# Decoder trunk with a top-2-of-8 expert layer: five steps of the last expert move behind the branch, and a small overflow block goes from two array tiles to four

## The chip, the cores and the metric

The kernel runs on one core of one Trainium2 chip. The time is in device microseconds (us) of one execution of the program; of several runs the median is given. A profile of one execution says what each engine did and when: PE is TensorE's matmul, PEld its weight load, DVE VectorE, ACT ScalarE, POOL GpSimd, and SP issues the weight loads (DMA).

## The reference

Two decoder layers work on 256 tokens of width 1024, all in float32. Each layer mixes tokens (mLSTM beside a short gated convolution) and then channels: a dense SwiGLU in the first layer, eight experts in the second. The change touches only the experts:

```python
logits = (t @ w_router).astype(jnp.float32)
top_v, top_i = lax.top_k(logits, TOP_K)
probs = jax.nn.softmax(top_v, axis=-1)
gates = (jax.nn.one_hot(top_i, N_EXPERTS, dtype=jnp.float32) * probs[..., None]).sum(-2)
out = jnp.zeros_like(t)
for e in range(N_EXPERTS):
    out = out + gates[:, e, None].astype(t.dtype) * swiglu(t, w13[e], w2[e])
```

with `swiglu(h, w13, w2) = (silu(a) * b) @ w2`, where `a` and `b` are the halves of `h @ w13`. Every expert has 3584 hidden columns: 29 MB of `w13` and 15 MB of `w2`. So the layer reads 352 MB of weights, whatever the routing.

## The kernel before

**Units, steps, parts.** Weights come in units of 1 MB (128 x 2048 float32), each loaded by SP into one buffer of a ring of seven (`load`, L112). An expert is worked in seven steps of 512 hidden columns. A step has two up parts (a and b, two units each) and a down part (two units). In a light expert the two up parts are one ("up", four units).

**Two ways to multiply.** An expert with up to 128 tokens is *wide* ("split"): ACT rounds each half unit to float32r (`hi`, L119), DVE takes the remainder (`lo`, L121), and TensorE makes three passes of 512 columns (L472 to L474). A *light* expert with up to 64 tokens is "plain": its weights are used raw in float32, and `side_by_side` (L1068) puts two matmuls beside each other in the array, each with 64 tokens as rows of the result and one half of the columns. A float32 matmul shows as two instructions in the trace. The activations are turned by TensorE (L1103), and a finished expert is scaled and added to the sum (`combine`, L1139 to L1151).

**Which expert goes which way.** The last expert (here e7) does not wait for the ranking: it runs wide, all seven steps, ahead of a branch (L1385), while DVE ranks the other seven by load. The branch chooses one of six ways from these loads. The profiled program takes the first: e0, the most loaded, has more than 128 tokens, so 128 of them are a wide block and the rest, the *overflow*, a second block of 64 slots with two array tiles; e1 is wide; e2 to e6 are light. For each of e0's half units the wide passes and the overflow's matmuls follow each other, on the same weights.

**What sets the order.** `ranked` (L1307) writes one list of parts: light parts, with heavy ones (e0, then e1) put in after light down parts by a cost per part, 4 for e0's and 1 for e1's, spread to the end. This gives the order of loads, conversions (up to five half units ahead) and matmuls in the program; the compiler's scheduler still moves instructions of one engine against each other. The code after the branch exists once for every way.

Of the kernel before, what the change touches and what calls it, by code (L numbers as in the profile page):

```python
# [14 lines left out]
OP = mybir.AluOpType  # L15
# [18 lines left out]
AHEAD = 4  # L34
NR = NE - 1
# [9 lines left out]
def trunk(ctx: ExitStack, tc: tile.TileContext, x, c, w_ada, b_ada, w_in, w_gates, b_gates, conv_qk,  # L45
# [85 lines left out]
    using = [None]  # L131


    def fits():
        live = [x[2] for x in loaded] + [x[3] for x in made if x[3]] + [x for x in using if x]
        return bool(plan) and (not live or loads[0] + 1 - min(live) < len(turns["raw"][1]))
# [685 lines left out]
    def moe(ctx, norms, gb, Gc, Bc, l, g1):  # L822
# [30 lines left out]
        slots = [const.tile([128, 128], F32, name=f"slots{i}") for i in range(3)]  # L853
# [3 lines left out]
        G.iota(slots[2].rearrange("p (a b) -> p a b", a=2), pattern=[[0, 2], [1, 64]], base=-int(OFF),  # L857
               channel_multiplier=0, allow_small_or_imprecise_dtypes=True)
# [62 lines left out]
        def order():  # L921
# [38 lines left out]
            V.scalar_tensor_tensor(most, most, 5.0, few[:, 0:1], op0=OP.mult, op1=OP.add)  # L960
# [23 lines left out]
        class Block:  # L984
            def __init__(self, hi, lo, place, ready=None):
                self.hi, self.lo, self.place, self.side, self.ready = hi, lo, place, lo is None, ready
# [79 lines left out]
        def side_by_side(o, act, w, n, start, stop):  # L1066
            for c in range(2):
                T.matmul(o[c * 64:c * 64 + 64, 0:n], act, w[:, c * n:c * n + n], start=start, stop=stop)  # L1068

        def activations(b):  # L1070
            if b.side:
                return small.tile([128, 256], F32, tag="ss", bufs=4, name="ss")
            return small.tile([128, 512], F32, tag="ms", bufs=2, name="ms")


        def up(xs, s):
# [3 lines left out]
            for k2, (whi, wlo, raw) in enumerate(w for _ in range(2) for w in unit(3)):  # L1080
                for b, src in zip(xs, srcs):
                    for kk in range(2):
                        k = k2 * 2 + kk
                        if b.side:
                            side_by_side(src, b.hi[:, k], raw[:, kk], 256, k == 0, k == KC - 1)
                        else:
                            passes(src, b.hi[:, k], b.lo[:, k], whi[:, kk], wlo[:, kk], k == 0, k == KC - 1)
# [9 lines left out]
        def turned(xs, s):  # L1097
            out_ = []
            for b, s_ in zip(xs, s):
# [4 lines left out]
                if b.lo is None:  # L1104
                    ghi, glo = small.tile([128, n, 128], F32, tag="mg", bufs=3, name="mg"), None
# [8 lines left out]
        def ybanks(xs):  # L1114
            return [bank() if b.side else [bank(), bank()] for b in xs]

        def down(xs, j, ys, gs_):
            for u in range(2):
                for kk, (whi, wlo, raw) in enumerate(unit(3)):
                    cc, first, last_ = u * 2 + kk, j == 0 and u + kk == 0, j == STEPS - 1 and u + kk == 2  # L1120
                    for b, y, (ghi, glo) in zip(xs, ys, gs_):
                        if b.side:

                            side_by_side(y, ghi[:, kk, u * 64:u * 64 + 64], raw[:, 0], 512, first, last_)
                            continue
                        for hf_ in range(2):
                            hs = slice(hf_ * 512, hf_ * 512 + 512)
                            passes(y[hf_], ghi[:, cc], glo[:, cc], whi[:, 0, hs], wlo[:, 0, hs], first, last_)
                    if bits:
                        bits.popleft()()  # L1130
# [5 lines left out]
        def combine(b, y, gs, DT):  # L1136
            ys = next_ys()
            if b.side:
                V.scalar_tensor_tensor(ys[:, 0], y, gs, g1_halves, op0=OP.mult, op1=OP.mult)  # L1139
            for hf_ in range(0 if b.side else 2):  # L1140
                V.scalar_tensor_tensor(ys[:, hf_], y[hf_], gs, g1[:, hf_ * 512:hf_ * 512 + 512], op0=OP.mult,
                                       op1=OP.mult)

            def add(tb):
                pos_ = [bank() for _ in range(2)]
                for hf_, po in enumerate(pos_):
                    ps = slice(hf_ * 64, hf_ * 64 + 64) if b.side else slice(0, 128)
                    T.matmul(po, DT[ps, tb * 128:tb * 128 + 128], ys[ps, 0 if b.side else hf_], start=True, stop=True)
# [64 lines left out]
        def parts_of(*exs):  # L1213
            steps = [(ex, j) for ex in exs for j in range(STEPS)]
# [10 lines left out]
        def run(parts, at):  # L1225
# [7 lines left out]
            for ex, j, what in parts:  # L1233
# [5 lines left out]
                if what in ("up", "up b"):  # L1239
# [3 lines left out]
                    if (ex, j) in at:  # L1243
                        at[ex, j]()
            bits_left(0)
# [40 lines left out]
        g1_halves = h4("g1_halves", F32, (128, 512))  # L1286
# [3 lines left out]
        for c in range(2):  # L1290
            A.copy(g1_halves[c * 64:c * 64 + 64], g1[c * 64:c * 64 + 64, c * 512:c * 512 + 512])
# [13 lines left out]


        def ranked(x_0, x_6, narrow):  # L1307
            restore(early)
# [199 lines left out]
```

## Time and profile before

| what | value |
|---|---|
| median of 3 runs | 1810.29 us (1809.36 to 1810.42) |
| profiled execution | 1809.25 us, span of its instructions 1807.5 us |
| granted TensorE clock, mean | 0.987 |
| TensorE busy | 1714.5 us (95%) |
| DVE / ACT busy | 1046.7 / 727.4 us |
| read from memory | 538.20 MB, 298 GB/s over the span |
| expert weights | 336 loads of 1024 KB on SP's queue |

A row of a group reads: line, engine, operation, what is written from what, shapes, count, then busy time, mean of one in ns, and the idle time ahead of it with its cause. Matmuls are pipelined: a row's length is that of one instruction through the array, and the next one starts before it ends, so throughput is read from the distance between starts.

### The profile page before, as it was taken

The numbers are of one execution on the slowest core, as the hardware profiler recorded it, in microseconds if no ns is written. First come the engines' busy times: TensorE is split into PE (matmuls) and PEld (weight loads), VectorE is DVE, ScalarE is ACT, GpSimd is POOL, SyncE is SP. The second block draws the span as 40 slices with busy tenths as digits, with TensorE's granted clock in tenths as the row PEclk, the third lists the DMA queues.
The fourth block names the chain that finished last, engine by engine and source line by source line (L and its number), as shares of the span: only waits on it lengthen the run. The fifth ranks groups of instructions, "written<-read, shape, count | busy, mean of one in ns | idle before, by whom it ended". The sixth has DMA issues, their size and how long they took to land. (4 is left out here: it accounts for less than half of the span.)

```text
span 1807.5 us, 27089 instructions
## 1 busy us (share of the span) xinstructions
PE 1714.5 (95%) x10848; PEld 1285.7 (71%) x10848; DVE 1046.7 (58%) x1524; ACT 727.4 (40%) x971; POOL 69.8 (4%) x80
## 2 busy tenths in 40 slices
PE   5999998999998999997999999999999999999996
PEld 4899996999996999995776555454554455566763
DVE  7699857866659999669887112222222222364645
ACT  2764544444434855446765112122121211244541
POOL 0002002000003001002000000000000000000000
PEclk8999999999999999998999999999999999999998
DMA  8666753866664677654886999999998999999993
GB/s 347 214 255 243 270 184 115 307 252 231 232 234 176 235 277 282 231 187 152 338 292 234 367 411 369 386 352 400 364 398 318 394 366 381 404 372 415 421 421 149
DMA packets 78126, 541.10 MB, mean 299 GB/s; under 512 B 10056, under 2 KB 10408, under 8 KB 13224
## 3 DMA queue, kind: packets, MB, share of 16 engines
q1 hardware_dynamic: 74880, 534.81, 76.3%
q10 hardware_dynamic: 3112, 4.48, 0.7%
q8 instruction: 87, 1.43, 0.3%
q14 instruction: 47, 0.39, 0.1%
HBM read 538.20 MB, written 1.05 MB: 298 GB/s over the span
## 5 line engine op out<-in xcount | busy, mean ns | idle before, releaser
L121 DVE TENSOR_TENSOR lo<-raw,hi 128x1024 fp32r<-128x1024 f32 x382 | 457.9, 1220 | 177.6 <-ACT hi L119 176.1
L119 ACT CAST hi<-raw 128x1024 fp32r<-128x1024 f32 x388 | 399.3, 1049 | 304.0 <-PE grp L461 184.2
L460 PE MATMUL grp<-h_hi,hi 128*128 128x256 f32 x1408 | 401.8, 286 | 0.5 <-ACT hi L119 0.5
L462 PE MATMUL grp<-h_hi,lo 128*128 128x256 f32 x1408 | 397.7, 283 | 0.0
L461 PE MATMUL grp<-h_lo,hi 128*128 128x256 f32 x1408 | 397.5, 282 | 0.0
L460 PEld LDWEIGHTS grp<-h_hi,hi 128*128 128x128 f32 x1408 | 268.6, 191 | 2.9 <-issue 1.4
L461 PEld LDWEIGHTS grp<-h_lo,hi 128*128 128x128 f32 x1408 | 268.6, 191 | 2.0 <-issue 1.7
L462 PEld LDWEIGHTS grp<-h_hi,lo 128*128 128x128 f32 x1408 | 268.4, 191 | 0.0
L1093 DVE TENSOR_TENSOR ss<-bank,ss 128x256 f32<-128x256 f32 x42 | 17.8, 425 | 308.8 <-PE bank L1068 301.4
L472 PE MATMUL bank<-hi,x_parts 128*128 128x512 f32 x336 | 138.9, 413 | 2.8 <-ACT hi L119 2.8
L474 PE MATMUL bank<-lo,x_parts 128*128 128x512 f32 x336 | 133.9, 399 | 1.8 <-DVE lo L121 1.8
L473 PE MATMUL bank<-hi,x_parts 128*128 128x512 f32 x336 | 132.2, 393 | 0.0
L1091 ACT ACTIVATE ss<-bank 128x256 f32<-128x256 f32 x42 | 16.1, 384 | 277.1 <-PE bank L1068 277.1
L1068 PE MATMUL bank<-raw,x_pairs 128*64 128x256 f32 x1024 | 117.1, 380 | 0.0
L1068 PE MATMUL bank<-raw,mg 128*64 128x512 f32 x432 | 115.7, 608 | 0.5 <-ACT mg L1106 0.5
L1068 PEld LDWEIGHTS bank<-raw,x_pairs 128*64 128x64 f32 x1024 | 72.4, 137 | 39.4 <-issue 3.7
L121 DVE TENSOR_TENSOR lo<-raw_moe,hi 128x1024 fp32r<-128x1024 f32 x76 | 89.9, 1219 | 16.7 <-ACT hi L119 15.9
L472 PEld LDWEIGHTS bank<-hi,x_parts 128*128 128x128 f32 x336 | 63.1, 188 | 39.4 <-issue 15.2
L119 ACT CAST hi<-raw_moe 128x1024 fp32r<-128x1024 f32 x76 | 77.5, 1049 | 22.2 <-PE bank L473 19.0
L273 DVE SCALAR_TENSOR_TENSOR acc<-raw,cond,acc 128x512 f32<-128x512 f32 x120 | 83.7, 744 | 0.1
L474 PEld LDWEIGHTS bank<-lo,x_parts 128*128 128x128 f32 x336 | 63.1, 188 | 20.7 <-DVE lo L121 6.5
L472 PE MATMUL bank<-hi,mg_hi 128*128 128x512 f32 x168 | 69.1, 419 | 4.9 <-ACT mg_hi L78 4.9
(309 smaller groups left out, 2304.2 us busy)
## 6 DMA issues: line engine op xcount, KB each, us to landing
raw<-in_moe_w_dram SPq DMA_DIRECT2D x192, 1024.0 KB, 8.6
raw_moe<-in_moe_w_dram SPq DMA_DIRECT2D x96, 1024.0 KB, 7.2
raw<-in_w_in_dram SPq DMA_DIRECT2D x72, 1024.0 KB, 5.7
raw<-in_w_ada_dram SPq DMA_DIRECT2D x48, 1024.0 KB, 4.8
raw_big<-in_moe_w_dram SPq DMA_DIRECT2D x48, 1024.0 KB, 9.2
raw<-in_dense_w_dram SPq DMA_DIRECT2D x42, 1024.0 KB, 4.6
raw<-in_w_out_dram SPq DMA_DIRECT2D x8, 1024.0 KB, 5.8
g<-in_b_ada_dram SPq DMA_DIRECT2D x8, 256.0 KB
```

Source lines behind the costliest of these rows:

```text
L119: A.copy(hi, raw)
L121: V.tensor_tensor(lo, raw, hi.bitcast(F32), op=OP.subtract)
L273: V.scalar_tensor_tensor(a, raw[:, jj], cond[:, j:j + 1], a, op0=OP.mult, op1=OP.add)
L460: T.matmul(o, whi[:, kk, fs], hi[:, k], start=first, stop=False, skip_group_check=True)
L461: T.matmul(o, whi[:, kk, fs], lo[:, k], start=False, stop=False, skip_group_check=True)
L462: T.matmul(o, wlo[:, kk, fs], hi[:, k], start=False, stop=k == KC - 1, skip_group_check=True)
L472: T.matmul(o, ahi, whi, start=start, stop=False)
L473: T.matmul(o, alo, whi, start=False, stop=False)
L474: T.matmul(o, ahi, wlo, start=False, stop=stop)
L1068: T.matmul(o[c * 64:c * 64 + 64, 0:n], act, w[:, c * n:c * n + n], start=start, stop=stop)
L1091: A.activation(dst, src, AF.Silu)
L1093: V.tensor_tensor(dst, src, dst, op=OP.mult)
```

## The change

1. The last expert runs only its first two steps ahead of the branch. Steps 2 to 6 are put at the head of the heavy parts behind it, among the light ones. Its two result banks (`ywide`) are now those of every wide block.
2. A new way comes first: if e0 has at most 160 tokens, the overflow is a block of 32 slots, and `side_by_side` puts four matmuls beside each other, each with 32 rows and a quarter of the columns. `combine` for such a block clears its tile on POOL and scales four pieces. Four small DVE operations make the new choice.
3. Where a part has a wide and a narrow block, the raw units are held until the part's end, and the overflow's matmuls are written after all wide ones of the part (`over_halves`).
4. The list starts with a light part, a part of e0 costs 3, and heavy parts are spread over all but the last four light parts.

```diff
-    using = [None]
+    using = []
...
-    def unit(parts=2):
+    def unit(parts=2, hold=False):
         for _ in range(2):
             convert_ahead(0, 1)
             w = made.popleft()
-            using[0] = w[3]
+            if w[3]:
+                using.append(w[3])
             yield w[0:parts]
-            using[0] = None
+            if w[3] and not hold:
+                using.remove(w[3])
             convert_ahead(lead[0])
...
+            least = const.tile([128, 2], F32, name="least")
+            V.tensor_scalar(least[:, 0:1], cs[:, 0:1], 160.0, None, op0=OP.is_le)
+            V.tensor_scalar(least[:, 1:2], few[:, 0:1], 0.0, None, op0=OP.is_equal)
+            V.tensor_tensor(least[:, 0:1], least[:, 0:1], least[:, 1:2], op=OP.mult)
+            V.scalar_tensor_tensor(few[:, 0:1], few[:, 0:1], 1.0, least[:, 0:1], op0=OP.add, op1=OP.subtract)
...
-        def side_by_side(o, act, w, n, start, stop):
-            for c in range(2):
-                T.matmul(o[c * 64:c * 64 + 64, 0:n], act, w[:, c * n:c * n + n], start=start, stop=stop)
+        def side_by_side(b, o, act, w, start, stop):
+            p, n = 128 // b.tiles, w.shape[1] // b.tiles
+            for c in range(b.tiles):
+                T.matmul(o[c * p:c * p + p, 0:n], act, w[:, c * n:c * n + n], start=start, stop=stop)
...
+        def over_halves(xs, n, wide, side):
+            both_ = len({b.side for b in xs}) > 1
+            kept = []
+            for i, (whi, wlo, raw) in enumerate(w for _ in range(n) for w in unit(3, both_)):
+                kept.append(raw)
+                if not xs[0].side:
+                    wide(i, whi, wlo)
+                elif not both_:
+                    side(i, raw)
+            if both_:
+                for i, raw in enumerate(kept):
+                    side(i, raw)
+                using.clear()
+                convert_ahead(lead[0])
...
         def ybanks(xs):
-            return [bank() if b.side else [bank(), bank()] for b in xs]
+            return [bank() if b.side else ywide if b is xs[0] else [bank(), bank()] for b in xs]
...
             ys = next_ys()
+            n = 1024 // b.tiles
+            if b.tiles == 4:
+                G.memset(ys, 0.0)
+            for c in range(2 if b.tiles < 4 else 4):
...
-        e_last = Expert(None, x_last)
-        run(parts_of(e_last), {(e_last, 2): lambda: x_first.extend(first_and_last())})
-        e0, e6 = Expert(w_r[0], [], "both"), Expert(w_r[NR - 1], [], "plain")
-        first = [(e0, 0, "up a"), (e0, 0, "up b"), (e6, 0, "up")]
+        ywide = [bank() for _ in range(2)]
+        e_last = Expert((units_of(moe_w13[last]), units_of(moe_w2[last])), x_last)
+        run(parts_of((e_last, 0, LAST_STEPS)), {(e_last, 0): lambda: x_first.extend(first_and_last())})
+        first = [(Expert(w_r[NR - 1], [], "plain"), 0, "up"), (e_last, LAST_STEPS, "up a")]
...
-            cost = [4 if len(e.xs) == 2 else 1 for e, _, _ in heavy_]
-            end = sum(cost) if narrow > 1 else sum(c for c, p in zip(cost, heavy_) if p[0] is ex[0])
-            order__, done, i = heavy_[0:2], sum(cost[0:2]), 2
+            cost = [3 if len(e.xs) == 2 else 1 for e, _, _ in heavy_]
+            end = sum(cost) if narrow > 1 else sum(c for c, p in zip(cost, heavy_) if p[0] in (e7[0], ex[0]))
+            order__, done, i = [], 0, 0
             for n, p in enumerate(light_):
                 order__.append(p)
-                while p[2] == "down" and i < len(heavy_) and done * len(light_) < end * (n + 2):
+                while (p[2] == "down" or not n) and i < len(heavy_) and done * (len(light_) - 4) <= end * n:
                     order__.append(heavy_[i])
                     done, i = done + cost[i], i + 1
...
-        ways = [lambda: ranked([x0, xx], [x6], 5), lambda: ranked([x0, xx], [x6], 3),
+        ways = [lambda: ranked([x0, xx.fewer(32, slots[3])], [x6], 5),
+                lambda: ranked([x0, xx], [x6], 5), lambda: ranked([x0, xx], [x6], 3),
```

The order of parts behind the branch is then, for each of the last expert's five steps, a light up, a light down and three heavy parts; for e0, one light up and one light down to each heavy part; for e1, again three heavy parts to a light step. Three places in the order of PE's instructions show it. Every row is a matmul of the program (`x4`: four in a row); `64x256` and `32x128` are rows and columns of a result tile.

**An up part of e0.** `x_pair` is the overflow's activation, `x_parts` the wide block's. Before:

```order
L1068 MATMUL bank<-raw_79,x_pair 64x256 x4
L472 MATMUL bank<-hi_83,x_parts_8388 128x512
L473 MATMUL bank<-hi_83,x_parts_8388 128x512
L474 MATMUL bank<-lo_90,x_parts_8388 128x512
L472 MATMUL bank<-hi_83,x_parts_8388 128x512
L473 MATMUL bank<-hi_83,x_parts_8388 128x512
L474 MATMUL bank<-lo_90,x_parts_8388 128x512
L1068 MATMUL bank<-raw_moe_7750,x_pair 64x256 x4
```

Now, the last wide run of such a part:

```order
L1085 MATMUL bank<-raw_big,x_pair 32x128
L478 MATMUL bank<-lo_94,x_parts_8167 128x512
L476 MATMUL bank<-hi_87,x_parts_8167 128x512
L477 MATMUL bank<-hi_87,x_parts_8167 128x512
L478 MATMUL bank<-lo_94,x_parts_8167 128x512
L476 MATMUL bank<-hi_83,x_parts_8167 128x512
L477 MATMUL bank<-hi_83,x_parts_8167 128x512
L478 MATMUL bank<-lo_90,x_parts_8167 128x512
L476 MATMUL bank<-hi_83,x_parts_8167 128x512
L477 MATMUL bank<-hi_83,x_parts_8167 128x512
L478 MATMUL bank<-lo_90,x_parts_8167 128x512
L1085 MATMUL bank<-raw_big,x_pair 32x128 x15
```

The overflow's matmuls are twice as many and half as large. They are not all behind the wide ones, as they are in the code: the scheduler has left wide runs of 2, 12 and 10 in this part, with 9, 8 and 15 tile matmuls behind them. Before, most runs were of 6.

**Right behind the branch.** Before, e0's wide passes come first:

```order
L1385 COMPARE_AND_BRANCH
L472 MATMUL bank<-hi_84,x_parts_8388 128x512
L473 MATMUL bank<-hi_84,x_parts_8388 128x512
L474 MATMUL bank<-lo_91,x_parts_8388 128x512
L472 MATMUL bank<-hi_84,x_parts_8388 128x512
L473 MATMUL bank<-hi_84,x_parts_8388 128x512
L474 MATMUL bank<-lo_91,x_parts_8388 128x512
L1068 MATMUL bank<-raw_82,x_pair 64x256 x4
```

Now a light up part (four units of e6, the least loaded), then the last expert's third step:

```order
L1459 COMPARE_AND_BRANCH
L1085 MATMUL bank<-raw_80,x_pair 64x256 x8
L1085 MATMUL bank<-raw_81,x_pair 64x256 x8
L1085 MATMUL bank<-raw_82,x_pair 64x256 x8
L1085 MATMUL bank<-raw_79,x_pair 64x256 x8
L476 MATMUL bank<-hi_84,x_parts_7855 128x512
L477 MATMUL bank<-hi_84,x_parts_7855 128x512
L478 MATMUL bank<-lo_91,x_parts_7855 128x512
```

`x_parts_7855` is the last expert's block: its remaining steps now share this stretch with the light parts, and e0 follows after five of them.

**The end.** Before, e1's last down part and the last light one run into each other (`ys,DT` are the matmuls that add a finished expert to the sum):

```order
L474 MATMUL bank<-lo_93,mg_hi 128x512
L1068 MATMUL bank<-raw_80,mg 64x512
L1068 MATMUL bank<-raw_81,mg 64x512
L1148 MATMUL bank<-ys,DT 128x512 x4
L1068 MATMUL bank<-raw_81,mg 64x512 x3
L1148 MATMUL bank<-ys,DT 128x512 x4
```

Now a whole light step stands behind e1's last matmul:

```order
L478 MATMUL bank<-lo_93,mg_hi 128x512
L1085 MATMUL bank<-raw_81,x_pairs 64x256 x4
L1085 MATMUL bank<-raw_82,x_pairs 64x256 x8
L1085 MATMUL bank<-raw_79,x_pairs 64x256 x8
L1085 MATMUL bank<-raw_moe_7750,x_pairs 64x256 x8
L1206 MATMUL bank<-ys,DT 128x512
L1085 MATMUL bank<-raw_moe_7751,mg 64x512 x2
L1206 MATMUL bank<-ys,DT 128x512
```

e1's addition lies among light matmuls there, and only the last light expert's is left behind them.

More of the change, by code (lines that the diff above doesn't have):

```diff
@@ L34 @@
 AHEAD = 4
+LAST_STEPS = 2
 NR = NE - 1
@@ L1079, in up, with wide, side @@
             srcs = [bank() for _ in xs]
-            for k2, (whi, wlo, raw) in enumerate(w for _ in range(2) for w in unit(3)):
+            def wide(k2, whi, wlo):
                 for b, src in zip(xs, srcs):
-                    for kk in range(2):
+                    for kk in range(0 if b.side else 2):
                         k = k2 * 2 + kk
[L1084 to L1087, printed above, removed]
+                        passes(src, b.hi[:, k], b.lo[:, k], whi[:, kk], wlo[:, kk], k == 0, k == KC - 1)
+            def side(k2, raw):
+                for b, src in zip(xs, srcs):
+                    for kk in range(2 if b.side else 0):
+                        k = k2 * 2 + kk
+                        side_by_side(b, src, b.hi[:, k], raw[:, kk], k == 0, k == KC - 1)
+            over_halves(xs, 2, wide, side)
             for src, dst in zip(srcs, s):
@@ L1114, in ybanks, with ends, a_bit, wide @@
         def ybanks(xs):
-            return [bank() if b.side else [bank(), bank()] for b in xs]
+            return [bank() if b.side else ywide if b is xs[0] else [bank(), bank()] for b in xs]
         def down(xs, j, ys, gs_):
[L1118 to L1130, printed above, removed]
+            def ends(cc):
+                return j == 0 and cc == 0, j == STEPS - 1 and cc == 3
+            def a_bit():
+                if bits:
+                    bits.popleft()()
+            def wide(cc, whi, wlo):
+                for b, y, (ghi, glo) in zip(xs, ys, gs_):
+                    for hf_ in range(0 if b.side else 2):
+                        hs = slice(hf_ * 512, hf_ * 512 + 512)
+                        passes(y[hf_], ghi[:, cc], glo[:, cc], whi[:, 0, hs], wlo[:, 0, hs], *ends(cc))
+                a_bit()
+            def side(cc, raw):
+                for b, y, (g, _) in zip(xs, ys, gs_):
+                    if b.side:
+                        n, p = g.shape[1], 128 // b.tiles
+                        side_by_side(b, y, g[:, cc % n, cc // n * p:cc // n * p + p], raw[:, 0], *ends(cc))
+                if xs[0].side:
+                    a_bit()
+            over_halves(xs, 2, wide, side)
         def next_ys():
@@ L1137, in combine @@
             ys = next_ys()
[L1138 to L1142, printed above, removed]
+            n = 1024 // b.tiles
+            if b.tiles == 4:
+                G.memset(ys, 0.0)
+            for c in range(2 if b.tiles < 4 else 4):
+                cs = slice(c * 512, c * 512 + 512) if b.tiles == 1 else slice(0, n)
+                ps = slice(c * 32, c * 32 + 32) if b.tiles == 4 else slice(0, 128)
+                src = y[c] if b.tiles == 1 else y[ps, cs]
+                dst = ys[ps, c * n // 512, c * n % 512:c * n % 512 + n] if b.tiles == 4 else ys[:, c]
+                if b.tiles == 2 and c:
+                    continue
+                g1_ = {1: g1, 2: g1_parts[:, 0], 4: g1_parts[:, 1]}[b.tiles][ps, cs]
+                V.scalar_tensor_tensor(dst, src, gs[ps], g1_, op0=OP.mult, op1=OP.mult)
             def add(tb):
@@ L1146, in add @@
                 for hf_, po in enumerate(pos_):
-                    ps = slice(hf_ * 64, hf_ * 64 + 64) if b.side else slice(0, 128)
-                    T.matmul(po, DT[ps, tb * 128:tb * 128 + 128], ys[ps, 0 if b.side else hf_], start=True, stop=True)
+                    ps = slice(hf_ * 64, hf_ * 64 + 64) if b.tiles == 2 else slice(0, 128)
+                    T.matmul(po, DT[ps, tb * 128:tb * 128 + 128], ys[ps, 0 if b.tiles == 2 else hf_], start=True,
+                             stop=True)
                 for hf_, po in enumerate(pos_):
@@ L1210, in part_units, with parts_of @@
                     + (rows_of(w2, j * 2, 2, ex.kind) if what == "down" else []))
-        def parts_of(*exs):
-            steps = [(ex, j) for ex in exs for j in range(STEPS)]
+        def parts_of(*runs):
+            steps = [(ex, j) for ex, j0, j1 in runs for j in range(j0, j1)]
             out_ = []
@@ L1343, in general @@
         def general():
+            e7 = rest_of_last()
             for q in (plan, loaded, made):
                 q.clear()
-            using[0] = None
+            parts = parts_of(e7)
+            plan.extend(u for p in parts for u in part_units(*p))
+            run(parts, {})
             lead[0] = 0
```

51 lines of the change are left out of this document (32 added, 19 removed).

## The prediction

> **What bounds the kernel now.** First the page: busy shares, then the slices for TensorE (PE), the transfers and their rate.
>
> ```profile
> PE 1714.5 (95%) x10848; PEld 1285.7 (71%) x10848; DVE 1046.7 (58%) x1524; ACT 727.4 (40%) x971; POOL 69.8 (4%) x80
> PE   5999998999998999997999999999999999999996
> GB/s 347 214 255 243 270 184 115 307 252 231 232 234 176 235 277 282 231 187 152 338 292 234 367 411 369 386 352 400 364 398 318 394 366 381 404 372 415 421 421 149
> ```
>
> PE is at nine tenths almost throughout, but a matmul's row runs on past the start of the next, so the spacing of starts is what counts below. The rate never passes 421 and differs a lot from slice to slice. Then the expert layer by stage: the last expert alone, the most loaded expert e0 among the light ones, the second one e1 among them, the end (columns: length, busy PE, PEld, DVE, ACT, POOL, clock, DMA share, GB/s).
>
> ```profile
> 840.00:980.00 140.00, 132.63 (x604) 105.52 (x603) 117.55 (x141) 99.63 (x114) 0.00 (x0) 1.00 0.82 308
> 980.00:1575.00 595.00, 580.33 (x3560) 309.52 (x3558) 149.26 (x204) 118.19 (x185) 0.00 (x0) 1.00 0.93 371
> 1575.00:1775.00 200.00, 193.98 (x1046) 128.04 (x1044) 114.82 (x121) 91.82 (x106) 0.00 (x0) 1.00 0.99 407
> 1775.00:1807.50 32.50, 17.09 (x54) 7.46 (x50) 16.12 (x28) 0.00 (x0) 1.97 (x2) 0.76 0.12 46
> ```
>
> PE is idle for 5, 2 and 3% of the first three stages, while the transfers run at 308, 371 and 407 GB/s. Who waits for whom settles it; the first row is the load queue's, the second the conversion's (us in total, times, longest), from 1000 us on:
>
> ```profile
> SPq L112 <- PE bank L1068: 462.1, 215, 5.9
> ACT hi L119 <- DMA raw<-in_moe_w_dram: 14.1, 10, 6.8
> ```
>
> Loads wait for PE to free a buffer far more than anything waits for a load. So PE sets the end, and the weights are the next bound close behind.
>
> **What a part of e0 costs.** An up part before (columns: start, length, operation):
>
> ```profile
> 1094.85 0.50 PE L472 MATMUL bank<-hi,x_parts 128*128 128x512 f32 x1
> ...
> 1099.81 1.08 PE L1068 MATMUL bank<-raw,x_pair 128*64 128x256 f32 x8
> 1100.83 0.50 PE L472 MATMUL bank<-hi,x_parts 128*128 128x512 f32 x1
> 1101.16 0.39 PE L473 MATMUL bank<-hi,x_parts 128*128 128x512 f32 x1
> 1101.39 0.40 PE L474 MATMUL bank<-lo,x_parts 128*128 128x512 f32 x1
> 1101.62 0.40 PE L472 MATMUL bank<-hi,x_parts 128*128 128x512 f32 x1
> 1101.86 0.39 PE L473 MATMUL bank<-hi,x_parts 128*128 128x512 f32 x1
> 1102.09 0.40 PE L474 MATMUL bank<-lo,x_parts 128*128 128x512 f32 x1
> 1102.41 1.08 PE L1068 MATMUL bank<-raw,x_pair 128*64 128x256 f32 x8
> ...
> 1105.92 3.62 PE L1068 MATMUL bank<-raw_moe,x_pair 128*64 128x256 f32 x32
> 1109.38 1.90 PE L1068 MATMUL bank<-raw_big,x_pair 128*64 128x256 f32 x16
> ```
>
> Wide passes start 0.2325 us apart (1101.16 to 1102.09 in four). In a pure run of half tiles (64 rows of the result each) an instruction starts every (1109.38 - 1105.92) / 32 = 0.108 us. One period of eight plus six takes 2.60 us (1099.81 to 1102.41), where 8 x 0.108 + 6 x 0.2325 = 2.26. The difference, **0.34 us, is the price of one wide run set among tiles**, in and out.
>
> The up part (32 overflow and 24 wide instructions) takes 11.07 us (1094.85 to 1105.92); its wide matmuls fall into five runs. A down part of e0 starts and ends here:
>
> ```profile
> 1071.69 0.50 PE L472 MATMUL bank<-hi,mg_hi 128*128 128x512 f32 x1
> ...
> 1082.29 1.08 PE L1068 MATMUL bank<-raw,mg 128*64 128x512 f32 x4
> 1083.20 0.60 PE L1068 MATMUL bank<-raw,x_pair 128*64 128x256 f32 x4
> ```
>
> That is 11.5 us. A step of e0 has two up parts and a down part: 33.6 us, and seven steps 236 us.
>
> **The four tiles.** An overflow instruction now carries 32 rows and streams half as many columns, and there are twice as many of them. No row of the trace shows four tiles; both bounds come from neighbours. How fast short instructions can follow each other, each with a weight load of its own, the router's counting shows:
>
> ```profile
> 831.07 0.17 PE L907 MATMUL bank<-mask,ones_b 128*128 128x8 bf16 x1
> 831.10 0.17 PE L907 MATMUL bank<-mask,before 128*128 128x8 bf16 x1
> ```
>
> Two half tiles overlap now: where every instruction of 256 columns starts 0.108 us after the one before, two side by side share 0.216, so 128 columns need 0.108. A chunk of the contraction is four instructions now, 0.43 us, and will be eight (four tiles, two passes each). If four tiles overlap as two do, it takes 2 x 0.108 = 0.21 us. If they do not overlap at all, 8 x 0.108 = 0.86. Four starts in 0.108 us ask for one every 0.027; the two rows are 0.03 apart, so the issue is just fast enough. I take 0.21, since the half tiles, the nearest row, reach their full factor of two; the far end stays as a rival. Down is the same sum: four chunks of twice the columns.
>
> The tiles of a part thus cost 8 x 0.21 = 1.7 us (before 3.5). The new code holds raw weights so that the overflow could run after all wide passes, but the order of instructions shown above does not keep this: wide matmuls still stand in three runs in an up part, three to four in a down part. So 24 x 0.2325 + 1.7 + 3 x 0.34 = 8.3 us, plus 0.2 for going from quarter to half tiles (my estimate, half a run's price): **8.5 us instead of 11.07**, and 8.7 instead of 11.5 in a down part. Over 21 parts: 14 x 2.57 + 7 x 2.8 = 55 us saved.
>
> The Trainium skill says in "TensorEngine Tiling (Array Packing)", section "Key Properties", that a change of tiling mode drains the array. The 0.34 us per run agrees; by that rule quarter to half tiles is a change too.
>
> **The moved steps.** Five steps of the last expert leave the stage where it stands alone. Rows: that stage, its gather, a combining of one expert (eight matmuls), a full cycle of e1 with one light step, and a light step alone.
>
> ```profile
> 839.40:980.00 140.60, 133.23 (x607) 106.03 (x606) 118.05 (x142) 100.23 (x115) 0.00 (x0) 1.00 0.81 307
> 839.40:980.00 140.60, 8.41 (x64) 8.53 (x64) 1.00 0.81 307
> 1784.54 3.70 PE L1148 MATMUL bank<-ys,DT 128*128 128x512 f32 x8
> 1719.90:1748.86 28.96, 28.34 (x160) 19.60 (x159) 15.55 (x15) 13.93 (x16) 0.00 (x0) 1.00 1.01 420
> 1083.20:1094.90 11.70, 11.08 (x85) 5.76 (x81) 2.54 (x3) 3.85 (x6) 0.00 (x0) 1.00 0.92 350
> ```
>
> Alone, a step costs (140.6 - 8.4 - 3.7) / 7 = 18.4 us, because the turning of its activations has little to cover it; among light parts 28.96 - 11.70 = 17.3. Five steps save 5.5 us. Their 30 loads move behind the branch on SP's queue with them, and the conversions (DVE busy 15.55 of 28.96 us in such a cycle) have room. The branch comes after two steps plus the gather, near 839 + 2 x 18.4 + 8.4 = 885 us. What it needs was ready long before:
>
> ```profile
> 840.07 0.15 DVE L961 CAST ints<-most 128x1 int32<-128x1 f32 x1
> 846.61 0.16 DVE L970 TENSOR_TENSOR gate_x<-gate_x,px 128x2 f32<-128x2 f32 x1
> ```
>
> Four small DVE operations for the new choice (0.15 each) lie before 840 and are covered by some 45 us. Were that cover gone, they would cost 0.6.
>
> **Small terms.** The overflow's combining now uses all 128 rows per matmul: 3.70 instead of the 1.99 us that the same eight take on half the rows, once; its four scalings of a quarter each are bounded by four of the present 0.75 us on DVE, which has slack. I add 2 us. Clearing its tile on POOL is bounded by POOL's 2.35 us for an operation of that size, in idle time there. Four light parts alone at the end replace e1 and a light part ending together: the last wait of the light expert (0.84) stays, e1's own last waits get cover, and nothing is booked.
>
> ```profile
> 819.12 2.35 POOL L376 TENSOR_TENSOR xA<-z,lng 128x1024 f32<-128x1024 f32 x1
> 1790.94 1.99 PE L1148 MATMUL bank<-ys,DT 64*128 64x512 f32 x8 [0.84 <-DVE ys L1139]
> ```
>
> **Do the weights keep up?** The layer's 336 units are of 1.05 MB each:
>
> ```profile
> raw<-in_moe_w_dram SPq DMA_DIRECT2D x192, 1024.0 KB, 8.6
> raw_moe<-in_moe_w_dram SPq DMA_DIRECT2D x96, 1024.0 KB, 7.2
> raw_big<-in_moe_w_dram SPq DMA_DIRECT2D x48, 1024.0 KB, 9.2
> ```
>
> At the branch 18 are issued, 318 are left: 318 x 1.0486 MB / 421 GB/s = 792 us, done at 1677. By the forecast PE ends near 1740 (its last matmul now ends at 1792.9, 14.6 us before the span does), so it asks for about 390 GB/s on average. Locally it asks for more: 12 units in 28.96 us are 434, above the 420 that came, and an e0 step with three light steps asks 24 units in 3 x 11.7 + 25.7 = 61 us, 413. Seven buffers are 17 us of supply; the five cycles of the last expert draw 5 x 0.9 = 4.5 of it. A part of e0 holds two of seven for its 8.5 us, which leaves five for the transfers. I add 5 us for weights that are late here and there (nothing to 17).
>
> **Sum**, against the profiled span of 1807.5: -55 - 5.5 + 2 + 5 = 1754. The profiled run's time is 1.75 us above its span, and the median of the runs shown 1.04 above that: **1757 us**, 2.9% faster.
>
> **Rivals.**
>
> *Four tiles overlap in part.* The parts hold 8 x 14 + 8 x 7 = 168 chunks (a down chunk counted twice). A quarter of the way from 0.21 to 0.43, 0.27 us, takes back 168 x 0.055 = 9 us: 1766. For: eight pairs at the rows' 0.03 us are already 0.24. Against: two tiles reach their full factor. The Trainium skill, "TensorE: Matmul & The Clock Gate", section "Measured speedup vs the span model", reports 2.38 times for three column tiles, 0.79 per tile; at that factor four give the same 0.27.
>
> *Four tiles are no faster than two* (0.43 us a chunk: the doubled instruction stream binds). For it: the needed 0.027 us is at the edge of what a row shows. Against: the weight loads and starts of two tiles fall together now. Only runs are saved, 14 x 0.85 + 7 x 1.1 = 19 us: 1807.5 - 19 - 5.5 + 2 + 2.8 = 1788.
>
> *Tiles do not overlap at all, slower.* A chunk at 0.86 us makes an up part 13.7 us, 2.6 more than before, a down part 2.4 more: 53 us, 1860. The point from which the change loses: 54 us more than forecast, 54 / 168 = 0.32 above 0.21, so 0.53 us a chunk, a tile instruction every 0.066 us. Against: two tiles overlap in every row.
>
> *The weights become the bound.* If the queue, with two buffers held in each e0 part, gives no more than the 371 GB/s of that stage, 318 units take 899 us; with 21 us from the last landing to the end (a light down part 3.7, its combining 2.8, then 14.6) that is 885 + 899 + 21 = 1805, 1808 as a median: no change. At 385 GB/s it is 1775. For: DMA share is 0.93 there. Against: the loads' waits are PE's.
>
> *The change doesn't do what it says*: with over 160 tokens for e0 the old way would run in the new order, near 1800. The reference's own routing, worked out from its seeded inputs, gives e0 132 tokens, four of overflow.
>
> **Chances.** Forecast 0.55 (own range 1743 to 1772: the saving between 50 and 62, weights late 0 to 17), overlap in part 0.12, no faster tiles 0.12, weights 0.12 (half of it within 0.2%, which is about what a measurement of this kernel can tell from no change), slower 0.06, other way 0.03. The range of 1738 to 1803 leaves out the slower case, the end of the weights' case and a tail below. Faster: 0.55 + 0.12 + 0.12 + 0.06 + 0.03 = 0.88; same 0.06; slower 0.06.
>
> **What would show it.** Right: four-tile rows of 128 columns start on average every 0.027 us, e0 parts of 8.5 us, e0's stage near 400 GB/s with PE still without waits for conversions. Wrong: a spacing of 0.05 or more; waits of PE or ACT for raw weights of tens of us; a wide run that costs more than 0.34 among quarter tiles; a branch later than 885 us.

## The result and the profile after

The median after is 1767.68 us (four runs, 1764.21 to 1769.47), beside 1809.82 us before on the same chip (1809.28 to 1810.42): a ratio of 0.9765, 95% interval 0.9748 to 0.9782, or 42 us less. The profiled execution took 1764.21 us, with a span of 1762.5 against 1807.5 before. The runs of the change lie on two levels, near 1765 and near 1769, and the profiled one is of the lower, so differences of a few us are read from spans below and differences of medians are named as such.

The page after (busy shares, then the transfer rate in 40 slices):

```profile
PE 1669.0 (95%) x11401; PEld 1282.6 (73%) x11401; DVE 1047.1 (59%) x1531; ACT 719.6 (41%) x975; POOL 70.6 (4%) x82
GB/s 342 222 250 267 263 181 123 283 249 253 229 236 123 286 268 256 242 229 107 263 330 416 411 397 376 373 403 380 352 419 364 393 393 411 392 366 421 421 420 175
```

The share of PE is the same 95%, with 45 us less of it. The stages are now the last expert's two steps, its other five among light parts, e0, e1, and the end (length, busy PE, PEld, DVE, ACT, POOL, clock, DMA share, GB/s):

```profile
840.00:887.00 47.00, 43.79 (x216) 35.86 (x213) 37.48 (x63) 31.53 (x45) 0.00 (x0) 0.96 0.67 246
887.00:1035.00 148.00, 144.58 (x847) 98.25 (x846) 73.27 (x95) 60.83 (x81) 0.00 (x0) 1.00 1.00 406
1035.00:1535.00 500.00, 483.46 (x3651) 279.73 (x3651) 167.32 (x207) 126.12 (x183) 0.95 (x1) 1.00 0.96 386
1535.00:1730.00 195.00, 187.53 (x1034) 126.11 (x1034) 105.76 (x110) 82.12 (x99) 0.00 (x0) 1.00 0.99 406
1730.00:1763.00 33.00, 16.55 (x76) 5.55 (x72) 14.59 (x26) 0.37 (x1) 1.97 (x2) 0.83 0.23 90
```

Transfers now run at 386 to 406 GB/s in all three stages behind the branch. Who waits, from 1000 us on for the load queue and for ACT's conversion:

```profile
SPq L114 <- PE bank L1085: 389.5, 189, 8.7
ACT hi L121 <- DMA raw<-in_moe_w_dram: 3.8, 3, 3.2
```

Loads still wait for PE, and the conversions wait for loads even less than before (14.1 us then). PE's own waits for conversions from 885 us on are small:

```profile
PE bank L476 <- ACT hi L121: 2.8, 2, 1.4
...
PE bank L478 <- DVE lo L123: 2.6, 4, 1.3
```

That is 5.4 us in all. The profile before has 4.1 from the same time on, so these waits grew by 1.3 us:

```profile
PE bank L472 <- ACT hi L119: 2.3, 3, 1.4
PE bank L474 <- DVE lo L121: 1.8, 3, 1.1
```

An up part of e0 after:

```profile
1420.35 0.47 PE L476 MATMUL bank<-hi,x_parts 128*128 128x512 f32 x1
...
1420.99 0.84 PE L1085 MATMUL bank<-raw_moe,x_pair 128*32 128x128 f32 x18
1421.76 0.50 PE L478 MATMUL bank<-lo,x_parts 128*128 128x512 f32 x1
...
1424.73 0.65 PE L1085 MATMUL bank<-raw_moe,x_pair 128*32 128x128 f32 x16
1425.30 0.50 PE L478 MATMUL bank<-lo,x_parts 128*128 128x512 f32 x1
...
1427.84 1.07 PE L1085 MATMUL bank<-raw_moe,x_pair 128*32 128x128 f32 x30
1428.84 1.52 PE L1085 MATMUL bank<-raw_big,x_pairs 128*64 128x256 f32 x12
```

It takes 8.49 us (1420.35 to 1428.84), where one took 11.07 before. Thirty instructions of the four tiles (1427.84 to 1428.84) take 1.00 us, change of tiling included: one every 0.033 us. Its wide matmuls still fall into three runs.

### The profile page after: what moved, and what is told of

It reads as the page before. It is cut to its first block, busy times and chain, and to the rows that moved or that the text cites. A ratio compares the mean times of both kernels' runs of the same rounds, so it can differ in the third digit from the quotient of the medians.

```text
span 1762.5 us, 28144 instructions
## 1 busy us (share of the span) xinstructions
PE 1669.0 (95%) x11401; PEld 1282.6 (73%) x11401; DVE 1047.1 (59%) x1531; ACT 719.6 (41%) x975; POOL 70.6 (4%) x82
## 5 line engine op out<-in xcount | busy, mean ns | idle before, releaser
L123 DVE TENSOR_TENSOR lo<-raw,hi 128x1024 fp32r<-128x1024 f32 x376 | 449.7, 1220 | 162.7 <-ACT hi L121 162.2
L121 ACT CAST hi<-raw 128x1024 fp32r<-128x1024 f32 x382 | 389.8, 1048 | 273.3 <-PE grp L465 177.5
L1132 DVE TENSOR_TENSOR ss<-bank,ss 128x256 f32<-128x256 f32 (+1 forms) x42 | 16.9, 402 | 236.7 <-PE bank L1085 236.7
L1130 ACT ACTIVATE ss<-bank 128x256 f32<-128x256 f32 (+1 forms) x42 | 15.4, 366 | 288.7 <-PE bank L1085 288.7
L1085 PE MATMUL bank<-raw,x_pairs 128*64 128x256 f32 x1056 | 122.4, 385 | 0.0
L1085 PE MATMUL bank<-raw,mg 128*64 128x512 f32 (+1 forms) x432 | 85.6, 537 | 0.5 <-ACT mg L1145 0.5
L1145 ACT COPY mg<-bank 128x256 f32<-128x256 f32 (+1 forms) x42 | 14.9, 355 | 158.3 <-PE bank L1142 158.3
```

The lines of the kernel that those rows point to most:

```text
L121: A.copy(hi, raw)
L123: V.tensor_tensor(lo, raw, hi.bitcast(F32), op=OP.subtract)
L1085: T.matmul(o[c * p:c * p + p, 0:n], act, w[:, c * n:c * n + n], start=start, stop=stop)
L1130: A.activation(dst, src, AF.Silu)
L1132: V.tensor_tensor(dst, src, dst, op=OP.mult)
```

## The experiments

The open questions: how much of the 42 us is the four tiles, how much the order of the overflow behind the wide passes ("the hold": raw weights are held to the part's end), how much the move of the last expert's steps; and whether PE's stream of instructions alone sets the time. In the expectations, theory P is that it does; rival W is that late weights set it in part, and that the move pays by spreading their demand. Ratios are to the kernel before in the same series of runs, since the series ran on several chips and its median lies between 1809 and 1813 us in them.

### The change again

> The changed kernel as it is, as the base for the others. Both theories say 1764 to 1770 us. Theory P (PE's instruction stream alone sets the time): PE waits for loads or conversions for less than 10 us behind the branch in this execution too. Theory W (the 11 us that are missing against the forecast went to weights that come late): an execution near 1769 shows 5 us or more of waits for weights than the first profile, whose time was 1764.2.

Measured: 1769.21 us (1763.6 to 1769.49), ratio 0.9770 (0.9755 to 0.9784), span 1763.5. The result stands. PE's waits for conversions are 5.4 us again, as theory P has it; this execution took 1765.3 us, so what one near 1769 does differently was not seen, and W's sign was not put to the test.

### Tiles and hold, apart: three kernels

Two tiles in place of four, hold kept (`two_tiles`):

```diff
-        ways = [lambda: ranked([x0, xx.fewer(32, slots[3])], [x6], 5),
+        ways = [lambda: ranked([x0, xx], [x6], 5),
```

> The overflow goes back to 64 slots in two array tiles; moved steps, held raw units and order stay. Theory P: the four tiles carry the gain. 168 chunks at 0.43 instead of 0.21 us are 36 us more, less some 4 us because light parts follow in the same tiling: about 1800 us, near the kernel before. Theory W: the move of the last expert's steps evens the demand for weights and carries 25 us or more of the gain: below 1785 us.

Four tiles, hold undone (`no_hold`); and with both edits (`two_no_hold`), only the move and the new order of parts are left:

```diff
-            for i, (whi, wlo, raw) in enumerate(w for _ in range(n) for w in unit(3, both_)):
+            for i, (whi, wlo, raw) in enumerate(w for _ in range(n) for w in unit(3)):
...
-                elif not both_:
+                if xs[0].side or both_:
                     side(i, raw)
-            if both_:
-                for i, raw in enumerate(kept):
-                    side(i, raw)
-                using.clear()
-                convert_ahead(lead[0])
```

> Overflow block in four tiles as in the change, but its matmuls are written right behind each half's wide passes, as before the change, and the raw weights of a half are let go with the half. Theory P (TensorE's stream alone sets the time): the change saves in two ways that add up, fewer columns per chunk (two tiles 1795.95 against four 1767.68, so 28) and fewer stretches of wide work among tiled work (the rest, 14). Without the second the time is 1767.7 + 14 = about 1782, 1776 to 1788, and e0's up part takes about 9.3 us in place of 8.5. Rival H (the held-back order matters only together with two tiles, or not at all, since the scheduler mixes the matmuls again anyway): 1762 to 1772. Rival W (holding the raw weights for a whole part delays loads, so letting them go early helps): below 1762.

> Both undone: two tiles of 64 slots, written right behind each half's wide passes. What is left of the change is the move of the last expert's steps 2 to 6 behind the branch and the split of the light parts between the two ends. Theory P: the move is worth nothing measurable (all_before 1766.38 against 1767.68), so this is the kernel before again, 1803 to 1812. Rival M (the move is worth something when TensorE has more to do per expert): 1797 or less.

| | hold undone (5 wide runs in an up part) | hold (3 wide runs) |
|---|---|---|
| two tiles | 1815.28 us, ratio 1.0021 (1.0010 to 1.0032) | 1795.95 us, ratio 0.9926 (0.9911 to 0.9942) |
| four tiles | 1780.61 us, ratio 0.9824 (0.9808 to 0.9841) | 1767.68 us, ratio 0.9765 (0.9748 to 0.9782) |

Two up parts carry the reading. With four tiles and no hold, start and end, with the short run of tiles between:

```profile
1434.35 0.48 PE L476 MATMUL bank<-hi,x_parts 128*128 128x512 f32 x1
...
1439.48 0.41 PE L1085 MATMUL bank<-raw_moe,x_pair 128*32 128x128 f32 x2
...
1443.66 1.51 PE L1085 MATMUL bank<-raw_big,x_pairs 128*64 128x256 f32 x12
```

With two tiles and no hold:

```profile
1461.78 0.47 PE L476 MATMUL bank<-hi,x_parts 128*128 128x512 f32 x1
...
1472.84 1.47 PE L1085 MATMUL bank<-raw_big,x_pairs 128*64 128x256 f32 x12
```

9.31 us and 11.06 us, with five wide runs each, against the 8.49 us with three. So two wide runs cost 0.82 us in a part of four tiles, **0.41 us a run** where the prediction took 0.34. By the ratios times 1810, the tiles are worth 29 us with the hold and 36 without, the hold 11 us with four tiles and 17 with two: most of the gain is the tiles, and the two overlap by some 6 us. The up part without the hold was expected at 9.3 us, and is 9.31. What is left without both edits is 0.2% slower than before, a little above the range of theory P: the move and the new order of parts gain nothing by themselves. With two tiles and the hold, 1795.95 is near the 1800 of theory P, and W's time (under 1785) fails too. Rival H, that the hold does nothing since the scheduler mixes the matmuls again, falls.

### All seven steps ahead of the branch

```diff
-LAST_STEPS = 2
+LAST_STEPS = 7
```

The first list of loads behind the branch (`first`) then names e0's up part.

> All seven steps of the last expert lie ahead of the branch again; four tiles, held units and the rule that spreads parts stay (the list behind the branch starts with a light up part and e0's first). Theory P: by the first profile of the changed kernel the moved steps gain 1.5 us, by the prediction 5.5 us: 1769 to 1773 us. Theory W: without the moved steps e0's stage asks for more weights than come: 15 us or more slower, with waits of PE or ACT for raw weights.

Measured: 1766.38 us (1763.83 to 1769.67), ratio 0.9767 (0.9751 to 0.9783), span 1762.4 against 1762.5 of the change: the same as the change, a little under P's range and far from W's. The runs spread too far for 1 or 2 us to be seen by the medians, and the same edit was made once more below, in a kernel whose runs lie closer.

### The written order kept

The overflow's matmuls of e0's parts are told to keep their place in the program, behind all wide ones (`pinned`):

```diff
-                T.matmul(o[c * p:c * p + p, 0:n], act, w[:, c * n:c * n + n], start=start, stop=stop)
+                m = T.matmul(o[c * p:c * p + p, 0:n], act, w[:, c * n:c * n + n], start=start, stop=stop)
+                if pinned[0]:
+                    tc.keep_in_program_order(m)
```

> In a part with a wide and an overflow block the overflow's matmuls keep the order of the code on PE, so each part has one wide run instead of three or four and no tile matmul stands alone. Theory P: an up part falls from 8.5 to 5.6 + 1.7 + 0.34 + 0.2 = 7.8 us, a down part from 9.25 to 7.8: 14 x 0.7 + 7 x 1.4 = 20 us less, about 1748 us. Theory W: weights already set the pace in e0's stage, so less than a third of it arrives: above 1761 us, and PE waits instead.

Measured: 1744.64 us (1743.32 to 1748.47), ratio 0.9645 (0.9630 to 0.9660), span 1743.2, so 19 us less than the change by the spans (23 by the medians): the 20 of theory P, and not the third or less of W. An up part and a down part of e0 in it:

```profile
1406.53 0.48 PE L476 MATMUL bank<-hi,x_parts 128*128 128x512 f32 x1
...
1412.27 1.95 PE L1087 MATMUL bank<-raw_moe,x_pair 128*32 128x128 f32 x64
1414.16 1.08 PE L1087 MATMUL bank<-raw_big,x_pairs 128*64 128x256 f32 x8
```

```profile
1173.87 0.51 PE L476 MATMUL bank<-hi,mg_hi 128*128 128x512 f32 x1
...
1179.67 1.93 PE L1087 MATMUL bank<-raw,mg 128*32 128x256 f32 x32
1181.53 3.67 PE L1087 MATMUL bank<-raw,x_pairs 128*64 128x256 f32 x32
1185.04 3.62 PE L1087 MATMUL bank<-raw_moe,x_pairs 128*64 128x256 f32 x32
```

One wide run each: 7.63 us for the up part, 0.86 less than with three runs (0.43 a run), and 7.66 for the down part. The 64 tile instructions of the up part take 1.89 us in all, 0.030 us each with the change of tiling; the half tiles' 32 of twice the columns take 3.51 (1181.53 to 1185.04). Four tiles so reach close to their full factor over two. Set beside the run of 16 in the up part of the change (0.57 us, 1424.73 to 1425.30), 48 more instructions take 1.32 us, so one of them takes 0.0275 us without the change of tiling, and a chunk of eight 0.22. PE's waits for `lo` grow from 2.6 to 6.5 us in this kernel. A down part of the change shows what the scheduler's mixing costs:

```profile
1177.78 1.07 PE L1085 MATMUL bank<-raw,mg 128*32 128x256 f32 x16
...
1181.77 0.62 PE L1085 MATMUL bank<-raw,mg 128*32 128x256 f32 x2
1182.32 0.50 PE L476 MATMUL bank<-hi,mg_hi 128*128 128x512 f32 x1
...
1183.45 0.62 PE L1085 MATMUL bank<-raw,mg 128*32 128x256 f32 x2
...
1187.05 0.65 PE L1085 MATMUL bank<-raw,x_pairs 128*64 128x256 f32 x4
```

One matmul for one tile (two instructions) among wide ones takes 0.55 us (1181.77 to 1182.32) where in a long run two instructions take 0.12 (1.86 us for 32). There are two such places here, and the part takes 9.27 us (1177.78 to 1187.05).

### Four buffers for the transposed gates

The profile after shows a half clock in the middle of e0, which the profile before does not. PE's rows at that place, then the windows of 1 us there (columns as in the table of stages):

```profile
1339.70 0.33 PE L1074 MATMUL bank<-ident,Gt 128*128 128x128 f32 x1
1340.47 0.33 PE L1074 MATMUL bank<-ident,Gt 128*128 128x128 f32 x1 [0.45 <-DVE Gt L1073]
1341.99 0.30 PE L1074 MATMUL bank<-ident,Gt 128*128 128x128 f32 x1 [1.19 <-DVE Gt L1073]
1342.22 0.93 PE L1085 MATMUL bank<-raw,x_pairs 128*64 128x256 f32 x4
1343.09 0.47 PE L1074 MATMUL bank<-ident,Gt 128*128 128x128 f32 x1
```

```profile
1342.00:1343.00 1.00, 1.00 (x5) 0.30 (x5) 0.35 (x1) 0.00 (x0) 0.00 (x0) 0.73 1.05 344
1343.00:1344.00 1.00, 1.00 (x7) 0.50 (x7) 0.40 (x2) 0.00 (x0) 0.00 (x0) 0.50 0.84 319
1344.00:1345.00 1.00, 1.00 (x8) 0.62 (x6) 0.61 (x3) 0.00 (x0) 0.00 (x0) 0.50 0.40 164
1345.00:1346.00 1.00, 1.00 (x10) 0.55 (x8) 0.00 (x0) 0.00 (x0) 0.00 (x0) 0.57 0.29 123
```

Each transpose of the gates waits for DVE, which waits for the one buffer of tile `Gt`; e0's two blocks need four in a row. The clock is at one half for some 3.4 us there. The edit:

```diff
-                t = small.tile([128, 128], F32, tag="Gt", bufs=1, name="Gt")
+                t = small.tile([128, 128], F32, tag="Gt", bufs=4, name="Gt")
```

> The change with four buffers in place of one for the transposed gates (tile Gt), nothing else. In the profile after, TensorE waits 3.8 us for VectorE at this tile, 2 us of it in one place (1339.7 to 1342.2 us), and behind that place the granted clock stands at one half for 3.4 us, which costs about 1.7 us more. Theory: the stall and with it the half clock vanish, 3 to 5 us less: 1763 to 1766 by the median of the runs with the change at 1767.68, and no 1-us stretch from 900 to 1700 us shows a clock of 0.50. Rival: the wait only moves to the matmuls in front of which the transposes stand, 1766 to 1770, and the half clock stays or comes at another place. If the runs of the change at 1769 are those in which such a stretch of half clock comes twice, gt4 shows one level of times only.

Measured: 1755.40 us (1755.23 to 1755.69), ratio 0.9689 (0.9673 to 0.9705), span 1753.5. The four transposes stand together now, and no window of 1 us from 900 to 1700 us is below 0.95 of the clock:

```profile
1336.92 0.66 PE L1074 MATMUL bank<-ident,Gt 128*128 128x128 f32 x4
1337.51 3.67 PE L1085 MATMUL bank<-raw,x_pairs 128*64 128x256 f32 x32
```

The direction was right and the size too small: 9.0 us by the spans (12.3 by the medians) for an expected 3 to 5. PE's waits, after and with four buffers, tell part of it:

```profile
PE bank L1074 <- DVE Gt L1073: 3.8, 7, 1.2
...
PE bank L476 <- ACT mg_hi L80: 2.8, 3, 1.1
```

```profile
PE bank L476 <- ACT mg_hi L80: 0.7, 1, 0.7
```

Gt's 3.8 us are gone, 2.1 of `mg_hi` (the turned activations of the wide blocks, rounded) went with them, and the four windows above lack 0.27 + 0.50 + 0.50 + 0.43 = 1.7 us of clock: 7.6 of the 9.0. The scheduler also set other instructions in another order, so the rest is not placed. That Gt's stall spreads the runs of the change over 5 us was a guess that fell: the four runs of this kernel lie within 0.5 us, but those of three later kernels with the same four buffers do not (a run at 1741.03 beside four near 1736, one at 1762.51 beside three near 1757, and five from 1731.65 to 1737.73). What spreads them was not found.

### Both, and the light transposes kept in order as well

`pinned_turn` adds to `pinned` the four buffers, and keeps the light experts' transposes behind the next part's matmuls, to cover PE's 0.6 us waits for `ss`, the light experts' activations that these transposes turn.

```diff
-                    T.transpose(pt[:, cc], s_[:, cc * 128:cc * 128 + 128], ident)
+                    m = T.transpose(pt[:, cc], s_[:, cc * 128:cc * 128 + 128], ident)
+                    if b.lo is None:
+                        tc.keep_in_program_order(m)
```

> As pinned (the matmuls of the mixed parts' overflow block keep their written order), and the light experts' transposes, too, keep their written order, which is behind the next part's matmuls; and four buffers for tile Gt. In pinned's profile TensorE waits 11.9 us at these transposes for VectorE's activations, 21 times 0.57 us, and 3.0 us at Gt. Theory P: both waits are covered by the matmuls that stand ahead of them, 15 us less: 1728 to 1734 (pinned 1744.64). Rival W: the load of weights already runs at 395 to 414 GB/s in pinned, and takes the place as the bound: 1738 to 1744. Rival O: the transposes now stand at worse places (each switches between wide and tiled work once more), 1744 to 1755.

Measured: 1777.73 us, ratio 0.9808 (0.9792 to 0.9825), 33 us slower than `pinned`, worse than every theory had it. PE's waits in it, and one of the places:

```profile
PE bank L476 <- ACT hi L121: 35.1, 25, 1.4
PE bank L478 <- DVE lo L123: 13.4, 23, 1.3
```

```profile
1205.33 0.44 PE L1148 MATMUL bank<-ident,ss 128*128 128x128 f32 x2
1205.80 0.37 ACT L1153 COPY mg<-bank 128x256 f32<-128x256 f32 x1 [6.83 <-PE bank L1148]
1206.07 3.89 ACT L121 CAST hi<-raw 128x1024 fp32r<-128x1024 f32 x4
1207.17 0.50 PE L476 MATMUL bank<-hi,x_parts 128*128 128x512 f32 x1 [1.41 <-ACT hi L121]
```

The waits for `ss` are gone, and 48.5 us of waits for conversions stand in their place (6.5 in `pinned`). ACT copies the turned activations, waits 6.83 us for the late transposes to do so, and its next weights are queued behind that copy: 0.27 us after it starts it rounds them, and PE waits 1.41 us for the first. Covering 12 us on one engine made the other engine's queue late. The expectations had looked at PE's queue alone.

The waits are not the whole loss. The granted clock, a mean of 0.985 in `pinned`, is 0.978 here. Behind the branch `pinned` has one stretch of half clock, of 3.4 us, and this kernel has seven; two of the windows of 20 us that hold one:

```profile
1140.00:1160.00 20.00, 18.93 (x165) 12.69 (x167) 6.73 (x8) 4.47 (x7) 0.00 (x0) 0.91 0.92 374
1480.00:1500.00 20.00, 18.07 (x101) 10.69 (x97) 6.87 (x10) 5.51 (x8) 0.00 (x0) 0.91 1.01 424
```

From 885 us on PE waits 51.7 us in all against 26.6 in `pinned`, 25 more, and six more half clocks of 1.7 us each cost 10: together 35 of the 37 us between the spans (1779.8 and 1743.2).

`pinned_gt4`, without the transposes:

> pinned and gt4 in one kernel: the overflow block's matmuls of the mixed parts keep their written order, and the transposed gates have four buffers. Theory: the two gains lie at different places and add up, 1744.64 - (1767.68 - 1755.40) = 1732.4, taken as 1730 to 1735; TensorE waits for VectorE at Gt no more; no 1-us stretch from 900 to 1700 us at a clock near 0.50; and the runs lie within 1 us, since gt4's did and pinned's lay over 5 us. Rival W (weights become the bound, pinned's load already ran at 395 to 414 GB/s): 1738 or more. Rival O (part of gt4's gain was a chance of the order): 1735 to 1742, with runs that still lie 5 us apart.

Measured: 1736.19 us (1735.80 to 1741.03), ratio 0.9586 (0.9573 to 0.9600), span 1734.2. By the spans the two gains add up, 9.0 here (1743.2 to 1734.2) and 9.0 in `gt4`; by the medians 8.5 of 12.3 came, and the runs lie 5 us apart again, where the theory had them within 1 us. The theory's 1730 to 1735 is missed by 1.2 us, and both the time and the spread are what rival O said: the median of `gt4` had also gained from the narrow spread of its runs, by chance or by its order. Rival W's 1738 was not reached.

### The move and the light parts at the end, once more

Both edits in `gt4`, whose runs lie within 0.5 us: `gt4_all_before` has `LAST_STEPS = 7`, `gt4_tail` spreads the light parts to the end as before.

```diff
-                while (p[2] == "down" or not n) and i < len(heavy_) and done * (len(light_) - 4) <= end * n:
+                while (p[2] == "down" or not n) and i < len(heavy_) and done * len(light_) <= end * n:
```

> gt4 with all seven steps of the last expert ahead of the branch: the move of steps 2 to 6 undone alone, in a kernel whose runs lie within 0.5 us, so that 1 us can be seen. The prediction's price for the move: 5.5 us saved, so 1761 here (gt4 1755.40). By the trace of the change (29.1 us per 12 units among the light parts): 1.5 us saved, so 1757. Rival (the move is worth nothing or costs): 1755.5 or less.

> gt4 with the light parts spread to the end: len(light_) - 4 taken back to len(light_) in the planner's rule, so that the last light parts come among the heavy ones and not alone at the end. Theory P (TensorE's stream alone sets the time; the same parts in another order): within 3 us of gt4, 1752 to 1758. Rival D (the change's light parts alone at the end shorten the last chain, since a light part's combining is shorter): 1759 to 1764. Rival W (parts alone at the end, with only weights to wait for, are what the loads cannot follow): 1748 to 1752.

Measured: 1757.55 us (1757.24 to 1762.51; ratio 0.9706, 0.9691 to 0.9721) with the move undone, so the move saves 2 us here, give or take one (in the change itself the spans showed nothing). And 1752.96 us (1751.97 to 1753.63; ratio 0.9672, 0.9657 to 0.9687) with the light parts spread, so the four alone at the end cost 2.4 us; rival D falls. The intervals of the ratios overlap `gt4`'s in both cases, the single runs do not.

The last one, `pinned_gt4` with the light parts spread:

> pinned_gt4 with the light parts spread to the end, as in gt4_tail. Theory P: the gain of gt4_tail (1755.40 to 1752.96, 2.4 us) carries over, 1732 to 1735 (pinned_gt4 1736.19). Rival W: with the matmuls in written order the loads are already near their highest rate, and the order of parts decides when a load can start; then the time can go either way by more than that: below 1730 or above 1738.

Measured: 1733.72 us (1731.65 to 1737.73), ratio 0.9574 (0.9555 to 0.9592), span 1731.5: 2.5 us less, as forecast. This is the fastest kernel of the study, 34 us under the change.

## Why the prediction was right, point by point

**The time.** 1757 was forecast and 1767.68 measured, inside the likeliest case's own range (1743 to 1772). Against the spans the sum said 53.5 us and 45.0 came. The time alone would not have told the forecast from its rival of part overlap, whose 1766 lies nearer; the rows of the tiles decide between them, and then other terms have to account for the difference.

**PE sets the end: right.** The experiments that changed only PE's stream moved the time by about what PE's rows said, `pinned_turn` apart, where PE waited for conversions that ACT began late, and not for loads. The rival of the weights falls, and with it most of the term of 5 us for late weights: PE waits for no load directly, and 5.4 us for conversions in all, 1.3 more than before.

**Four tiles, 0.21 us a chunk: right.** Its 8.5 us for an up part met 8.49. The pieces were a little off against each other: a run costs 0.41 to 0.43, and the extra 0.2 for the next change of tiling was not needed beside that. The start spacing asked for, 0.027 us, came as 0.030 with the change of tiling in it and 0.0275 without (a chunk of 0.22 us, where part overlap had 0.27). The rivals of part overlap, no gain and no overlap fall. Two of the signs of being wrong did come, a wide run above 0.34 us among quarter tiles and a branch later than 885 us; both are sizes of terms, and neither changes what sets the time.

**The down part: mis-sized.** 8.7 was forecast and 9.27 came, so seven parts gave back some 4 of the 55 us. The step counted wide runs at one price; single tile matmuls at 0.55 us stood between them.

**The moved steps: mis-sized.** 5.5 us forecast, 2 measured in `gt4` and nothing in the change. The branch was to come at 885 us; the first matmul behind it is here:

```profile
887.51 2.81 PE L1085 MATMUL bank<-raw,x_pair 128*64 128x256 f32 x24
```

That is 2.5 us later. The forecast had 18.4 us for each step, a mean over seven; that two steps leave the gather less work to lie under is likely, but was not tried.

**Four light parts at the end: nothing was booked, they cost 2.4 us.**

**What the sum did not have.** The row of waits for Gt stood in the profile before as well, and its 3.0 us were left in the base. After the change the same waits at another place were followed by half a clock: 0.8 us more waiting and 1.7 us of clock.

Together: 4 (down) + 3.5 (move) + 2.4 (end) + 2.5 (Gt and clock) - 3.7 (weights, of which 1.3 of 5 came) = 8.7 us, beside the 8.5 between 45.0 and 53.5. The move and the end are differences of medians, good to 1 us or 2, so that the two sums lie so close is luck. The term for the weights, too large by 3.7, made the forecast look closer than its other terms were. The overflow's combining (2 us booked) was not tried apart.

## What to carry to other kernels

Price a mixed stream of TensorE by its changes of tiling and not by its columns alone: here two wide runs less in a part were worth 11 to 17 us, where halving the columns was worth 29 to 36. Look whether the order you write is the order that runs, and fix it where a matmul stands alone between two tilings; but before you fix an instruction's place, look at what is queued behind its consumer on the next engine. A wait of 2 us on the bounding engine can cost more than itself, so several short waits in a row deserve a second buffer first.

## What the runs showed of the hardware

- Four array tiles of 32 rows came within a tenth of their full factor over two: 64 instructions of 128 columns in 1.89 us, with the change of tiling, where 32 of 256 columns on half tiles take 3.51. The Trainium skill, "TensorE: Matmul & The Clock Gate", section "Measured speedup vs the span model", has 2.38 times for three column tiles over one, 0.79 a tile; four tiles over two come nearer to their full factor here (3.51 / 1.89 = 1.86).
- The clock fell to one half for about 3.4 us right behind a stretch of 2.3 us (1339.70 to 1341.99) in which PE did little but two short transposes. The Trainium skill, "TensorE: Matmul & The Clock Gate", section "What's actually happening", describes a free-running window of 3413 ns and a half clock after an idle one; the length agrees, while PE's idle stretch here was shorter than a window. In the kernel with two tiles and the hold, PE waits 3.0 us at Gt as in `pinned`, but no window of 1 us from 880 to 1760 us is below 0.95, where `pinned` has one half clock; so when such a stretch is punished and when not stays open.
- One tile's two instructions between wide matmuls took 0.55 us, over four times their share in a long run.
